# Value-product sums issued three half items earlier, the second dilated head held back until the values exist

## The chip, the cores and the metric

The kernel runs on one core of one Trainium2 chip. A core has a matrix engine (PE, TensorE), a vector engine (DVE), a scalar engine (ACT), a general engine (POOL) and an engine that issues DMAs (SP); each works through its own list of instructions in the order in which they stand there, and engines wait for each other by semaphores. The metric is the device time of one execution in microseconds (us), the median of several runs. Smaller is better.

## The reference

One decoder layer on x of 512 tokens by 1024 channels, in float32. A projection of x gives the queries, keys and values of three token mixers and three gates; the mixers' outputs are projected, gated, summed and projected again; a layer norm, an MLP with a gated embedding and a second layer norm follow. What matters here is the third mixer, dilated attention: 3 groups (g = 0, 1, 2) of 4 heads of 128 channels, combined over the groups by their softmax denominators.

```python
proj = x @ w_in
(da_q, da_k, da_v, sb_q, sb_k, sb_v, dl_q, dl_k, dl_v, gates) = jnp.split(proj, _split_points(), axis=-1)
...
o_dl = dilated_attention(dl_q.reshape(dil_shape), dl_k.reshape(dil_shape), dl_v.reshape(dil_shape),
                         rel_bias[:, DA_HEADS:])
...
# per group: logits = q k + bias, softmax over the window, o = prob @ v
wts = jax.nn.softmax(jnp.stack(lses, axis=0), axis=0)
o = wts[0][..., None] * outs[0] + wts[1][..., None] * outs[1] + wts[2][..., None] * outs[2]
```

## The kernel before

**Products in three parts.** A float32 operand is split into a high part (a rounded copy, made by ACT: lines 214 and 239) and a low part (the rest, made by DVE: lines 216 and 240). A product is then three matmuls: high by high, high by low, low by high. Weights come in chunks of 128x1024: SP loads a chunk into one of 7 buffers (`raw`), ACT makes `wh`, DVE makes `wl`, and PE uses them. There are 6 buffers each for `wh` and `wl`, so a chunk can be split only when PE is done with the chunk six places ahead of it.

**Items.** PE's main stream is a list of items, each a product over the whole depth with its weights. `item` records them, and the loop at the end of `trunk` goes through them. Between items, and once halfway through a whole item, the loop calls `step()`, which moves every unfinished attention head and every entry of `pending` on to its next `yield`. Half items (`size=0.5`), of which the values' products are made, have no halfway step. The place of a `yield` thus sets where the work after it is written among the items. From this written order a scheduling layer makes the final list of each engine, and it may move an instruction past others that do not depend on it. Tiles of 128x512 come out of one pool of 46 buffers (`slot`), so a tile may take the buffer of one that is no longer needed, and has to wait for its last reader.

**The values.** `value_pair` computes the dilated values of groups 1 and 2 with seven products in place of eight (Strassen's scheme, Winograd's form). They are numbered 1 to 7 and run in the order 2, 1, 7, 6, 4, 5, 3; each has two half items (r = 0, 1) of 12 matmuls. Products 2, 1 and 3 take x as it is. Products 7, 6, 4 and 5 take sums of blocks of x, which `value_forms` makes: it loads x again (`xr`, by POOL's DMA queue), waits some steps (`WAIT`), lets DVE form each sum in tiles `fr` (`o7`, `o6`, `o4`, `o1`, four instructions of 128x256 each), and `parts(p, ...)` splits it into a high part (`u7h`, ACT, line 239) and a low part (`u7l`, DVE, line 240). The sum called `o1` belongs to product 5, `o4` to product 4. Line 376 is the sum for 7, line 369 those for 6 and 4, line 388 that for 5.

**A dilated head.** `dil_head(hd)` is a generator, one for each of four heads. Head `hd` waits until its queries and keys of all three groups exist, then: the group 0 scores on PE (line 1589), DVE adds the bias and takes the maxima (1592), ACT takes the exponentials (1598); the scores of groups 1 and 2 (1605, 1613, 1620) likewise. Then each token's maxima and sums are exchanged between layouts by two small matmuls, `fold` (1630) and `foldT` (1632). On their output (`sel`, line 1636) DVE does a chain of small steps (1638 to 1652, with one exponential on ACT in it, 1647) which ends with the scaling of the exponentials (1654 and 1658). PE then transposes the scaled tiles (1673 for group 0, 1682 for groups 1 and 2), copies of them (`pt`) follow, and PE multiplies them by the values (1694, 1699). Before that last part a head waits for all values. Two heads can be under way together, since each counts 3 of 8 banks.

Of the kernel before, what the change touches and what calls it, by code (L numbers as in the profile page):

```python
# [57 lines left out]
def trunk(tc, a, out):  # L58
    nc = tc.nc
    es = ExitStack()  # L60
    with es:
# [14 lines left out]
        def slot(name, dt=F32):  # L76
            return big.tile([P, 512], dt, name=nm(name), tag="s", bufs=NSLOT)
# [176 lines left out]
        V = {}  # L254
# [89 lines left out]
        def form(to, p, r):  # L344
            fs = [split(r[kp], f"u{p}") for kp in range(2)]
            to[p] = [[fs[k // 2][i].rearrange("p (k t) -> p k t", k=2)[:, k % 2, :] for i in range(2)]
                     for k in range(4)]

        def value_forms():

            xr = [slot("xr") for _ in range(8)]
            for k, t in enumerate(xr):
                i = nc.gpsimd.dma_start(t, xt[:, k, :])
                tc.add_manual_dep(getattr(i, "ins", i), lows[-1].name, mybir.DependencyInfo(
                    mybir.DependencyClass.Sync, mybir.DependencyReason.DATA), reason="not ahead of time")

            def blk(kh, k, th):
                return xr[4 * kh + k].rearrange("p (t c) -> p c t", c=4)[:, 2 * th:2 * th + 2, :]

            def new():  # L360
                ts = [slot("fr") for _ in range(2)]
                return ts, [ts[k // 2].rearrange("p (k c t) -> p k c t", k=2, c=2)[:, k % 2] for k in range(4)]

            def parts(p, ts):
                form(vf, p, ts)
                vf[p] = [[(h[:, r * P:r * P + P], lo[:, r * P:r * P + P]) for r in range(2)] for h, lo in vf[p]]

            def neg_sub(o, i, j):
                nc.vector.scalar_tensor_tensor(o, i, -1.0, j, op0=OP.mult, op1=OP.subtract)

            for _ in range(WAIT):
                yield
            f7, o7 = new()
            with tc.issue_after(st["low"]):
                for k in range(4):
                    nc.vector.tensor_sub(o7[k], blk(1, k, 1), blk(0, k, 1))
            parts(7, f7)
            yield
            f6, o6 = new()
            with tc.issue_after(st["low"]):  # L380
                for k in range(4):
                    neg_sub(o6[k], o7[k], blk(0, k, 0))
            yield
            parts(6, f6)
            yield
            f1, o1 = new()
            for k in range(4):
                nc.vector.tensor_sub(o1[k], blk(0, k, 0), blk(0, k, 1))
            yield
            f4, o4 = new()  # L390
            for k in range(4):
                neg_sub(o4[k], o6[k], blk(1, k, 0))
            yield
            parts(4, f4)
            yield
            parts(5, f1)
            yield

        WAIT = 8

        def value_pair(nv):

# [1173 lines left out]
        def dil_head(hd):  # L1576
            while any(("dl_q", 4 * g + hd) not in T or ("dl_k", 4 * g + hd) not in T for g in range(3)):
                yield
            q = [T["dl_q", 4 * g + hd] for g in range(3)]
            k = [T["dl_k", 4 * g + hd] for g in range(3)]  # L1580
            stt = one.tile([P, 2, 8], F32, name=nm("st"), tag="st", bufs=4)
# [75 lines left out]
                o = L12[c // 2][:, (c % 2) * 256:(c % 2) * 256 + 256]  # L1657
                nc.vector.tensor_scalar(o, o, mxx[:, c:c + 1], None, op0=OP.mult)
            yield
            if hd < 2:  # L1660
                yield
                yield

# [48 lines left out]
        for hd in range(4):  # L1712
            waiting.append((3, dil_head(hd), DIL_PERIOD))
# [40 lines left out]
        for n, it in enumerate(items):  # L1754
# [4 lines left out]
            if n == v_from[0]:  # L1759
                pending.append(value_forms())  # L1760
# [182 lines left out]
```

## Time and profile before

| | |
|---|---|
| median of 3 runs | 1067.32 us (1067.2 to 1068.34) |
| the profiled execution | 1067.35 us, its span 1065.6 us |
| PE busy | 1049.0 us, 98% of the span |
| DVE busy | 774.1 us, 73% |
| ACT busy | 568.5 us, 53% |
| the values' seven products | from 238 to 295 us |
| dilated heads 0 and 1 | from 237 to 300 us; head 2 from 306, head 3 from 342 us |

Of the profile, three views are used. The table by stretches gives busy time of each engine in a stretch of time, with the granted clock of PE (PEclk, 1.00 is full) after the engines. The list of waits gives who waited for whom. The timeline gives instructions in order of time: start, duration, engine, line, operation, output and inputs, and in brackets how long the engine was idle before it and for whom it had waited. In the timeline a matmul of 128x512 has a duration near 0.4 us, but the next one starts 0.23 us after it: the starts tell how fast PE goes.

### The profile page before, as it was taken

The numbers are of one execution on the slowest core, as the hardware profiler recorded it, in microseconds if no ns is written. First come the engines' busy times: TensorE is split into PE (matmuls) and PEld (weight loads), VectorE is DVE, ScalarE is ACT, GpSimd is POOL, SyncE is SP. The second block draws the span as 40 slices with busy tenths as digits, with TensorE's granted clock in tenths as the row PEclk, the third lists the DMA queues.
The fourth block names the chain that finished last, engine by engine and source line by source line (L and its number), as shares of the span: only waits on it lengthen the run. The fifth ranks groups of instructions, "written<-read, shape, count | busy, mean of one in ns | idle before, by whom it ended". The sixth has DMA issues, their size and how long they took to land.

```text
span 1065.6 us, 15588 instructions
## 1 busy us (share of the span) xinstructions
PE 1049.0 (98%) x5802; PEld 905.1 (85%) x5802; DVE 774.1 (73%) x1383; ACT 568.5 (53%) x991; POOL 145.8 (14%) x224
## 2 busy tenths in 40 slices
PE   9999999999899999999999999999999999999996
PEld 6887788889788888888999988888999889889885
DVE  6887667649844757769768773888677877877965
ACT  6665445526432546547535452675756665666641
POOL 0001401220212103230111130100101100100000
PEclk9999999999899999999999999999999999999999
DMA  8346767974898819982676693148888978776602
GB/s 315 111 150 228 168 198 190 306 265 126 234 325 248 241 40 286 243 240 81 204 192 197 180 308 125 62 138 296 225 300 261 242 246 264 244 237 235 196 22 79
DMA packets 63260, 219.75 MB, mean 206 GB/s; under 512 B 7912, under 2 KB 8824, under 8 KB 63184
## 3 DMA queue, kind: packets, MB, share of 16 engines
q1 hardware_dynamic: 37056, 126.80, 34.1%
q0 software_dynamic: 25552, 91.04, 32.9%
q8 instruction: 45, 0.74, 0.3%
q10 hardware_dynamic: 576, 0.92, 0.2%
q14 instruction: 31, 0.25, 0.1%
HBM read 216.61 MB, written 81.81 MB: 280 GB/s over the span
## 4 chain that ended last, share of the span: by engine, by line
PE 88%; DVE 7%; issue 2%; ACT 2%; DMA 0%; POOL 0%; SPq 0%; DVEq 0%; POOLq 0%; ACTq 0%
PE mm L89 13%; PE mm L91 13%; PE mm L90 13%; PE at L89 4%; PE at L1076 4%; PE at L1077 4%; PE at L1078 4%; PE at L91 4%; PE at L90 4%; DVE wl L216 2%; PE mm L458 2%; PE mm L460 2%; PE mm L459 2%; PE at L133 1%; PE at L1467 1%
## 5 line engine op out<-in xcount | busy, mean ns | idle before, releaser
L214 ACT CAST wh<-raw 128x1024 fp32r<-128x1024 f32 x249 | 256.7, 1035 | 262.8 <-PE mm L90 158.7
L216 DVE TENSOR_TENSOR wl<-raw,wh 128x1024 fp32r<-128x1024 f32 x249 | 298.5, 1205 | 99.1 <-ACT wh L214 96.4
L89 PE MATMUL mm<-xhT,wh 128*128 128x512 f32 x368 | 146.7, 399 | 0.0
L91 PE MATMUL mm<-xhT,wl 128*128 128x512 f32 x368 | 144.4, 393 | 0.0
L90 PE MATMUL mm<-xlT,wh 128*128 128x512 f32 x368 | 144.0, 391 | 0.0
L91 PEld LDWEIGHTS mm<-xhT,wl 128*128 128x128 f32 x368 | 69.1, 188 | 15.0 <-DVE wl L216 0.3
L89 PEld LDWEIGHTS mm<-xhT,wh 128*128 128x128 f32 x368 | 69.2, 188 | 13.7 <-issue 0.4
L90 PEld LDWEIGHTS mm<-xlT,wh 128*128 128x128 f32 x368 | 69.2, 188 | 12.9
L1076 PE MATMUL at<-wh,hh 128*128 128x512 f32 x188 | 73.7, 392 | 0.0
L1077 PE MATMUL at<-wl,hh 128*128 128x512 f32 x188 | 73.7, 392 | 0.0
L89 PE MATMUL mm<-x1hT,wh 128*128 128x256 f32 x256 | 73.7, 288 | 0.0
L1078 PE MATMUL at<-wh,hl 128*128 128x512 f32 x188 | 73.1, 389 | 0.0
L90 PE MATMUL mm<-x1lT,wh 128*128 128x256 f32 x256 | 72.3, 283 | 0.0
L91 PE MATMUL mm<-x1hT,wl 128*128 128x256 f32 x256 | 71.9, 283 | 0.0
L89 PEld LDWEIGHTS mm<-x1hT,wh 128*128 128x128 f32 x256 | 48.8, 191 | 4.7 <-ACT up L1010 2.7
L90 PEld LDWEIGHTS mm<-x1lT,wh 128*128 128x128 f32 x256 | 48.9, 191 | 1.5
L914 POOL DMA_DIRECT2D usum<-in_wu_dram x32 | 28.5, 891 | 152.3 <-DVE wl L216 126.6
L91 PEld LDWEIGHTS mm<-x1hT,wl 128*128 128x128 f32 x256 | 48.6, 191 | 0.0
L914 POOL DMA_DIRECT2D dsum<-in_wd_dram x28 | 24.9, 890 | 130.9 <-DVE wl L216 96.2
L1078 PEld LDWEIGHTS at<-wh,hl 128*128 128x128 f32 x188 | 35.3, 188 | 7.7
L1076 PEld LDWEIGHTS at<-wh,hh 128*128 128x128 f32 x188 | 35.5, 189 | 6.0
L1077 PEld LDWEIGHTS at<-wl,hh 128*128 128x128 f32 x188 | 35.5, 189 | 5.5
(516 smaller groups left out, 2666.7 us busy)
## 6 DMA issues: line engine op xcount, KB each, us to landing
usum<-in_wu_dram POOLq DMA_DIRECT2D x48, 512.0 KB, 7.9
raw<-in_wt_dram SPq DMA_DIRECT2D x46, 512.0 KB, 5.1
dsum<-in_wd_dram POOLq DMA_DIRECT2D x42, 512.0 KB, 8.3
raw<-usum SPq DMA_DIRECT2D x32, 512.0 KB, 4.7
raw<-dsum SPq DMA_DIRECT2D x28, 512.0 KB, 4.5
raw<-in_wd_dram SPq DMA_DIRECT2D x25, 512.0 KB, 4.3
raw<-in_wu_dram SPq DMA_DIRECT2D x24, 512.0 KB, 5.2
raw<-in_wv_dram SPq DMA_DIRECT2D x18, 512.0 KB, 8.5
```

The costliest lines, as they stand in the source:

```text
L89: nc.tensor.matmul(ps, wh, xh, start=start, stop=False, skip_group_check=True)
L90: nc.tensor.matmul(ps, wh, xl, start=False, stop=False, skip_group_check=True)
L91: nc.tensor.matmul(ps, wl, xh, start=False, stop=stop, skip_group_check=True)
L214: i = nc.scalar.copy(h, raw)
L216: i = nc.vector.tensor_sub(lo, raw, h.bitcast(F32))
L458: nc.tensor.matmul(ps, x1, c["h"][:, s], start=k == 0, stop=False)
L459: nc.tensor.matmul(ps, x1, c["l"][:, s], start=False, stop=False)
L460: nc.tensor.matmul(ps, x2, c["h"][:, s], start=False, stop=k == 7)
L914: i = nc.gpsimd.dma_start(o, i, accum_op=OP.add, max_dma_last_dim=4096)
L1076: nc.tensor.matmul(ps, h[:, q], c["h"][:, s], start=go, stop=False, skip_group_check=True)
L1077: nc.tensor.matmul(ps, h[:, q], c["l"][:, s], start=False, stop=False, skip_group_check=True)
L1078: nc.tensor.matmul(ps, lo[:, q], c["h"][:, s], start=False, stop=end, skip_group_check=True)
```

## The change

Three edits. `WAIT` goes from 8 to 5, so `value_forms` starts three steps earlier. Inside it, the sum for product 4 and its split now come ahead of the sum for product 5. And head 1 of `dil_head` begins only when the last of the first pair's values exists; the two extra yields after the scaling, which heads 0 and 1 had, remain for head 0 alone.

```diff
             parts(6, f6)
             yield
+            f4, o4 = new()
+            for k in range(4):
+                neg_sub(o4[k], o6[k], blk(1, k, 0))
+            yield
+            parts(4, f4)
+            yield
             f1, o1 = new()
             for k in range(4):
                 nc.vector.tensor_sub(o1[k], blk(0, k, 0), blk(0, k, 1))
             yield
-            f4, o4 = new()
-            for k in range(4):
-                neg_sub(o4[k], o6[k], blk(1, k, 0))
-            yield
-            parts(4, f4)
-            yield
             parts(5, f1)
             yield
 
-        WAIT = 8
+        WAIT = 5
...
+            while hd == 1 and ("dl_v", 1, 3) not in V:
+                yield
...
-            if hd < 2:
+            if hd == 0:
                 yield
                 yield
```

The lines of `dil_head` from the new wait on are three higher afterwards (1632 becomes 1635, 1673 becomes 1676).

Where instructions now stand. The first place is DVE's list at the low part of the sum for product 4 (`u4l`). Before, it stands behind the chain of head 1 (`sel_2597` to `mxx_2602`, `ex_2604`):

```order
L369 SCALAR_TENSOR_TENSOR fr_2656<-fr_2480,xr_2186 128x256
L1643 TENSOR_TENSOR mxx_2602<-st_2459,ot_2599 128x8
L369 SCALAR_TENSOR_TENSOR fr_2656<-fr_2480,xr_2187 128x256
L1645 TENSOR_TENSOR ex_2604<-st_2459,mxx_2602 128x8
...
L216 TENSOR_TENSOR wl_2713<-raw_2294,wh_2712 128x1024
L1650 TENSOR_TENSOR mxx_2602<-mxx_2602,ex_2604 128x8
L240 TENSOR_TENSOR u4l_2692<-fr_2656,u4h_2691 128x512
```

Now it stands right behind the maxima of head 0 and ahead of that head's `foldT` operand (`r_517`), and all of `sel` and what follows comes later:

```order
L1626 TENSOR_TENSOR r_516_2475<-st_2408,exf 128x32
L240 TENSOR_TENSOR u4l_2480<-fr_2429,u4h_2479 128x512
L1620 TENSOR_SCALAR nm_2423<-st_2408 128x4
L216 TENSOR_TENSOR wl_2501<-raw_2051,wh_2500 128x1024
L240 TENSOR_TENSOR u4l_2484<-fr_2430,u4h_2483 128x512
L216 TENSOR_TENSOR wl_2507<-raw_2119,wh_2506 128x1024
L1629 TENSOR_TENSOR r_517_2477<-st_2408,exf 128x32
L436 TENSOR_TENSOR dl_v_2448<-dl_v_2448,mm_2548 128x512
L1639 TENSOR_TENSOR sel_2518<-at_2515,pick 128x64
L436 TENSOR_TENSOR dl_v_2512<-dl_v_2512,at_2573 128x512
L1641 TENSOR_REDUCE ot_2520<-sel_2518 128x2x4
```

The sums for product 4 have moved ahead of the work that they stood behind. The second place is PE's list at head 0's `foldT` (line 1632) and its first transposes (line 1673). Before, a product 1 half item less two matmuls (`mm_2577`), a whole one (`at_2627`) and one of product 7 (`mm_2662`, inputs `u7h` and `u7l`) stand between the two:

```order
L1632 MATMUL at_2514<-r_509_2457,foldT 128x32
L428 MATMUL mm_2577<-wh_2235,xlT 128x512
...
L1630 MATMUL at_2594<-r_536_2565,fold 128x32
L426 MATMUL at_2627<-wh_2235,xhT 128x512
...
L426 MATMUL mm_2662<-wh_2337,u7h_2407 128x512
...
L428 MATMUL mm_2662<-wh_2371,u7l_2412 128x512
L1673 MATMUL at_2678<-ident,L_490_2381 128x128 x3
```

Now both half items of product 1 and five of product 7's first twelve matmuls stand ahead of `foldT` (now line 1635), and seven matmuls stand between it and the transposes (now line 1676):

```order
L427 MATMUL mm_2602<-wl_2352,u7h_2331 128x512
L1635 MATMUL at_2515<-r_517_2477,foldT 128x32
L428 MATMUL mm_2602<-wh_2351,u7l_2332 128x512
L426 MATMUL mm_2602<-wh_2399,u7h_2335 128x512
L427 MATMUL mm_2602<-wl_2400,u7h_2335 128x512
L428 MATMUL mm_2602<-wh_2399,u7l_2336 128x512
...
L1676 MATMUL at_2618<-ident,L_502_2409 128x128 x3
```

The number of matmuls between `foldT` and the first transpose went from 34 to 7 (a small `fold` of head 1 aside). On DVE, between head 0's `sel` and its scaling (line 1657), there now stand one addition for product 1 and two weight chunks' low parts:

```order
L1639 TENSOR_TENSOR sel_2518<-at_2515,pick 128x64
L436 TENSOR_TENSOR dl_v_2512<-dl_v_2512,at_2573 128x512
L1641 TENSOR_REDUCE ot_2520<-sel_2518 128x2x4
L1643 TENSOR_REDUCE ot_2520<-sel_2518 128x2x4
L216 TENSOR_TENSOR wl_2587<-raw_2176,wh_2586 128x1024
L1646 TENSOR_TENSOR mxx_2523<-st_2408,ot_2520 128x8
L216 TENSOR_TENSOR wl_2593<-raw_2239,wh_2592 128x1024
L1648 TENSOR_TENSOR ex_2525<-st_2408,mxx_2523 128x8
```

Before, head 1's maxima (line 1613) and one low part stood there. The third place is PE's list behind the values, where head 1 now begins (`at_2871`) with head 2 right behind it (`at_2981`); before, head 1 was over by then and head 2 was there alone:

```order
L1592 MATMUL at_2871<-dl_k_1532,dl_q_1488 128x128
...
L1633 MATMUL at_2949<-r_619_2924,fold 128x32
L1592 MATMUL at_2981<-dl_k_2178,dl_q_2121 128x128
L1592 MATMUL at_2981<-dl_k_2178,dl_q_2121 128x256
L1592 MATMUL at_2982<-dl_k_2178,dl_q_2121 128x256 x2
L1635 MATMUL at_2949<-r_620_2926,foldT 128x32
L89 MATMUL mm_2997<-xhT,wh_2751 128x512
```

Head 1's `foldT` now stands behind head 2's first scores, and 20 matmuls of the next item (`mm_2997`) stand between it and head 1's transposes. From the fourth item behind the values on, PE's list is the same as before.

More of the change, by code (lines that the diff above doesn't have):

```diff
@@ L385, in value_forms @@
             yield
-            f1, o1 = new()
-            for k in range(4):
-                nc.vector.tensor_sub(o1[k], blk(0, k, 0), blk(0, k, 1))
-            yield
             f4, o4 = new()
@@ L395, in value_forms @@
             yield
+            f1, o1 = new()
+            for k in range(4):
+                nc.vector.tensor_sub(o1[k], blk(0, k, 0), blk(0, k, 1))
+            yield
             parts(5, f1)
             yield
-        WAIT = 8
+        WAIT = 5
         def value_pair(nv):
```

## The prediction

> **What bounds the kernel now.** I read the page's head first, then the list of PE's waits, then the timeline where those waits lie, then the table by stretches for the clock.
>
> ```profile
> span 1065.6 us, 15588 instructions
> PE 1049.0 (98%) x5802; PEld 905.1 (85%) x5802; DVE 774.1 (73%) x1383; ACT 568.5 (53%) x991; POOL 145.8 (14%) x224
> ```
>
> PE is busy 98% of the span: a change gains only where PE idles or runs slowly, and loses where it makes PE do so. The two longest of PE's waits stand in one place:
>
> ```profile
> PE mm L426 <- ACT u4h L239: 2.1, 1, 2.1
> PE mm L428 <- DVE u4l L240: 1.5, 1, 1.5
> ```
>
> PE waited for the high and the low part of the sum for product 4. The timeline of PE there, with earlier rows that serve as its prices:
>
> ```profile
> 258.77 0.93 PE L1673 MATMUL at<-ident,L 128*128 128x128 f32 x7
> 259.45 0.47 PE L426 MATMUL at<-wh,u7h 128*128 128x512 f32 x1
> ...
> 263.92 0.41 PE L1632 MATMUL at<-r,foldT 128*128 128x32 f32 x2
> 264.16 0.48 PE L428 MATMUL mm<-wh,u6l 128*128 128x512 f32 x1
> 264.48 0.39 PE L426 MATMUL mm<-wh,u6h 128*128 128x512 f32 x1
> 264.71 0.40 PE L427 MATMUL mm<-wl,u6h 128*128 128x512 f32 x1
> ...
> 266.08 0.40 PE L428 MATMUL mm<-wh,u6l 128*128 128x512 f32 x1
> 268.53 0.50 PE L426 MATMUL mm<-wh,u4h 128*128 128x512 f32 x1 [2.06 <-ACT u4h L239]
> 268.87 0.40 PE L427 MATMUL mm<-wl,u4h 128*128 128x512 f32 x1
> 270.78 0.79 PE L428 MATMUL mm<-wh,u4l 128*128 128x512 f32 x1 [1.52 <-DVE u4l L240]
> ...
> 276.36 0.38 PE L1682 MATMUL at<-ident,L 128*128 128x128 f32 x2
> ```
>
> Starts are 0.23 us apart (264.48 to 264.71), and seven transposes take 0.68 (258.77 to 259.45). From 266.08 to 276.36 PE did one matmul, the twelve of product 4's first half and seven transposes: 13 x 0.23 + 0.68 = 3.67 us of work in 10.28. So 6.6 us are lost there. Of these 2.2 and 1.7 are pauses (266.31 to 268.53, 269.10 to 270.78); the other 2.7 is a slow clock:
>
> ```profile
> 268.00:270.00 2.00, 0.73 (x2) 0.30 (x2) 2.00 (x6) 1.98 (x4) 0.00 (x0) 0.79 1.03 279
> 270.00:272.00 2.00, 1.22 (x3) 1.03 (x4) 2.00 (x7) 0.00 (x0) 1.65 (x2) 0.50 0.56 160
> ...
> 274.00:276.00 2.00, 2.00 (x8) 1.60 (x7) 1.25 (x4) 0.00 (x0) 0.00 (x0) 0.50 1.06 211
> 276.00:278.00 2.00, 2.00 (x17) 1.84 (x16) 1.44 (x3) 1.10 (x2) 0.00 (x0) 1.00 1.03 256
> ```
>
> The granted clock is 0.50 from about 269.2 (a mean of 0.79 over 2 us) to 276, some 6.8 us. DVE, busy for all 2.00 us of these stretches until 274, is what was late.
>
> **The change part by part.** It adds no work and removes none; it moves three things.
>
> *The sums earlier (8 to 5, and 4 ahead of 5).* By DVE's new order the sum for 4 and both its low parts stand right behind head 0's maxima, some twenty microseconds ahead of PE's use of them (268.53 above). The waits of 2.2 and 1.7 us go, and the slow clock that came of them: **-6.6 us**. What can be late next is the start: the earliest sum now stands in DVE's list behind the low part that ended at 227.1, and reads x loaded anew:
>
> ```profile
> 214.36 4.26 POOL L353 DMA_DIRECT2D xr<-in_xT_dram  x8 [5.74 <-DVE wl L216]
> ...
> DMA to landing us min/median/max: 5.2/6.1/7.2
> ...
> 225.91 1.23 DVE L216 TENSOR_TENSOR wl<-raw,wh 128x1024 fp32r<-128x1024 f32 x1 [0.17 <-ACT wh L214]
> 230.00:240.00 10.00, 10.00 (x46) 8.63 (x45) 4.32 (x11) 2.70 (x3) 1.37 (x2) 1.00 0.51 145
> ```
>
> The last xr is issued by 218.6 and lands by 225.8 at the slowest, 1.3 us ahead. The early sums cost nothing, since DVE is busy only 4.32 of the 10 us from 230; if the loads came later than 227.1, DVE would stand, but PE, with other operands in hand, not at once. No DMA is added, and the loads keep their place on POOL's queue; SP's loads follow DVE's low parts, most of which move by a microsecond or less.
>
> *Head 0 has its `foldT` later.* This is the new cost. `foldT` now stands behind both halves of product 1, and only seven matmuls separate it from the transposes that need DVE's whole chain. How long that chain is, heads 2 and 3 show:
>
> ```profile
> 316.40 0.31 PE L1632 MATMUL at<-r,foldT 128*128 128x32 f32 x2
> 320.46 1.14 PE L1673 MATMUL at<-ident,L 128*128 128x128 f32 x7
> ...
> 316.75 0.22 DVE L1636 TENSOR_TENSOR sel<-at,pick 128x64 f32<-128x64 f32 x1 [0.78 <-PE at L1632]
> 317.26 1.21 DVE L216 TENSOR_TENSOR wl<-raw,wh 128x1024 fp32r<-128x1024 f32 x1
> 318.39 0.16 DVE L1643 TENSOR_TENSOR mxx<-st,ot 128x8 f32<-128x8 f32 x1
> 320.03 1.08 DVE L1654 TENSOR_SCALAR L<-L,mxx 128x128 f32<-128x128 f32 x4
> ...
> 352.93 0.30 PE L1632 MATMUL at<-r,foldT 128*128 128x32 f32 x2
> 358.48 1.28 PE L1673 MATMUL at<-ident,L 128*128 128x128 f32 x7 [0.17 <-DVE L L1654]
> ...
> 265.02 0.70 DVE L436 TENSOR_TENSOR dl_v<-dl_v,at 128x512 f32<-128x512 f32 x1
> ```
>
> In head 2 it took 4.06 us from `foldT` (316.40) to the first transpose (320.46), with one foreign low part of 1.13 in it (317.26 to 318.39): 2.9 bare. In head 3 it took 5.55 with more strangers, and PE did wait, so such a chain sets PE's start. In the new order head 0's chain holds two low parts and one addition (0.65, from the row of 0.70 less its overlap): 2.9 + 2 x 1.13 + 0.65 = 5.8; some gaps between dependent small steps are filled by the strangers, which I put at 0.2: 5.6. PE meanwhile has `foldT` and the first matmul behind it (264.48 - 263.92 = 0.56) and six more at 0.23: 1.9. So PE stands **3.6 us**, ahead of the seven transposes. Bounds: 3.2 if the strangers fill more, 4.3 if `foldT`'s own operand, which now also follows the sum for 4 and two low parts, is late too. I take 3.6, from the sum.
>
> *The clock after it.* No row shows one pause of 3.6 us. Below, a pause that leaves the clock alone: 0. Above, 6.8 us at half clock all spent on work: 6.8 x 2.7 / 5.2 = 3.5, since the 5.2 us of slow work from 270.78 to 276 cost 2.7. The nearest row is that one, as the pauses total about the same (3.9 us against 3.6). I take **2.1**, a little less than 2.7, because the old pause came in two parts, and the clock could not begin to recover until 1.6 us after its drop (269.2 to 270.78), while unbroken work follows the new one.
>
> [...]
>
> *Head 1 behind the values.* Its work is the same but moves from a stretch where DVE is full to one where it is not:
>
> ```profile
> 300.00:310.00 10.00, 10.00 (x49) 8.44 (x49) 2.64 (x10) 2.59 (x6) 1.61 (x2) 1.00 1.05 353
> ```
>
> DVE is busy there 2.64 of 10 us. Head 1's own chain there holds one low part (1.13) and head 2's four maxima (about 1.3): 2.9 + 2.4 = 5.3, less 0.3 of filled gaps, 5.0. PE has 0.56 and 19 x 0.23 = 4.9 in that time. **+0.1**; bounds 0 and 1. There are also fewer changes between small and large matmuls on PE, each of which costs about 0.1 (264.16 to 264.48 is 0.32 in place of 0.23), some four fewer: **-0.4**. The two yields dropped for head 1 cost nothing, as its transposes lie where PE has the items' work; if that cover went, they would be part of the same 0.1. Waiting ahead of head 1 stand no instructions: the wait is one in the writing order, not on an engine. Heads 2 and 3 keep their turn.
>
> **Sum.** -6.6 + 3.6 + 2.1 + 0.1 - 0.4 = -1.2. The profiled execution took 1067.35 us (a span of 1065.6 and 1.75 around it), 0.03 above the median of the three runs. That gives 1066.1.
>
> **The rivals.** Same, within 0.2%, means within 2.1 us here, about what a measurement tells from no change.
>
> 1. *The new stall does not come:* head 0's scaling is done when PE reaches the transposes. It would need the chain in 1.9 us, and the bare one is 2.9 already; only if DVE or PE ran elsewhere than by their lists. Then -6.6 - 0.4 = -7.0: 1060.3. Chance 0.07.
>
> 2. *The stall comes, but the clock stays:* -1.2 - 2.1 = -3.3: 1064.0. For it speaks that a pause of 2.2 us alone preceded the old drop by less than one more us of work, so that a pair of pauses may have been needed; against it, that the new pause is longer than either. Chance 0.22.
>
> 3. *Slower: head 1 stalls PE behind the values as head 0 does.* Place: its transposes, 20 matmuls behind its `foldT`. The margin is nil (5.0 against 4.9), and head 2's first work sits in its chain. From 3.3 us more than I count it outweighs the gain and the bound of 2.1; a full repetition, a pause of 3.6 and a slow clock of 2.1, gives -1.2 + 5.7 = +4.5: 1071.9. Against it: DVE is three quarters idle there. Chance 0.13.
>
> 4. *The change does nothing:* the 6.6 us return elsewhere in full, as another wait for the sums. DVE's list speaks against it; it would be 1067.4, inside the same verdict. Chance 0.06.
>
> **How the numbers follow.** My forecast has 0.52, from 1064.9 (clock 1.0) to 1067.9 (clock 3.0, stall 4.3); a tenth of it counts as faster, the rest as same. Faster, below 1065.2: 0.07 + 0.22 + 0.05 = 0.34, to which I add 0.03 for small terms that all fall well, 0.37. Slower: 0.13 + 0.01. Same: 0.49. The range for 8 in 10 takes in rival 2 and part of 3: 1063.4 to 1068.6; the forecast's own is 1064.9 to 1067.9.
>
> **What would show it.** Right: no wait for `u4h` or `u4l` in PE's list; one wait of 3 to 4 us at the first transposes of head 0 near 255 to 259 us, for DVE's scaling, with `sel` 0.35 us behind `foldT` and two low parts in between; a granted clock of 0.50 for some microseconds after it; no wait above 0.5 us at heads 1 and 2. Wrong: a clock of 1.00 behind that pause takes 2.1 off, a second wait behind the values adds; and any wait in the first product 7 half would say that the early sums were not early enough.

## The result and the profile after

The changed kernel takes **1065.72 us** (median) against 1067.05 for the kernel before, each over 22 executions: a ratio of 0.999, with a 95% interval of 0.9983 to 0.9996. The forecast was 1066.1 with "within 0.2%" as the likeliest case, and the difference lies within that. The profiled execution took 1065.99 us, 1.36 less than that of before. One execution after (2100.37 us) and one of experiment 1 (1288.95 us) were in a slow state and stand in no ratio.

The head of the page after:

```profile
span 1064.3 us, 15603 instructions
PE 1046.7 (98%) x5802; PEld 903.7 (85%) x5802; DVE 776.6 (73%) x1383; ACT 568.9 (53%) x991; POOL 146.2 (14%) x224
```

In the list of PE's waits those for `u4h` and `u4l` are gone, and one of 3.5 us stands in their place:

```profile
PE at L1676 <- DVE L L1657: 3.7, 2, 3.5
```

PE's timeline around it (start, duration, line, output and inputs; the idle time before in brackets):

```profile
253.35 0.30 PE L1635 MATMUL at<-r,foldT 128*128 128x32 f32 x2
...
254.95 0.39 PE L428 MATMUL mm<-wh,u7l 128*128 128x512 f32 x1
258.88 1.14 PE L1676 MATMUL at<-ident,L 128*128 128x128 f32 x7 [3.54 <-DVE L L1657]
259.77 0.48 PE L426 MATMUL at<-wh,u7h 128*128 128x512 f32 x1
...
261.06 0.63 PE L427 MATMUL at<-wl,u7h 128*128 128x512 f32 x1
261.49 0.63 PE L428 MATMUL at<-wh,u7l 128*128 128x512 f32 x1
...
264.20 1.03 PE L1685 MATMUL at<-ident,L 128*128 128x128 f32 x8
264.99 0.48 PE L426 MATMUL mm<-wh,u6h 128*128 128x512 f32 x1
```

This is head 0: `foldT` at 253.35, its transposes at 258.88. After the pause matmuls start 0.43 us apart (261.06 to 261.49) in place of 0.23. From 254.95 to 264.99 PE did 13 matmuls, seven transposes and eight more (0.79): 2.99 + 0.68 + 0.79 = 4.46 us of work in 10.04. The loss is 5.6 us, 3.7 of it the pause (254.95 + 0.23 to 258.88). It replaces the old loss of 6.6.

What DVE did meanwhile:

```profile
253.69 0.22 DVE L1639 TENSOR_TENSOR sel<-at,pick 128x64 f32<-128x64 f32 x1 [0.79 <-PE at L1635]
253.83 0.68 DVE L436 TENSOR_TENSOR dl_v<-dl_v,at 128x512 f32<-128x512 f32 x1
...
254.66 1.22 DVE L216 TENSOR_TENSOR wl<-raw,wh 128x1024 fp32r<-128x1024 f32 x1
...
255.87 1.22 DVE L216 TENSOR_TENSOR wl<-raw,wh 128x1024 fp32r<-128x1024 f32 x1
...
258.45 1.07 DVE L1657 TENSOR_SCALAR L<-L,mxx 128x128 f32<-128x128 f32 x4
```

One addition and two low parts stand inside the chain from `sel` to the scaling. The granted clock (the third number from the end of each row, a mean over 2 us):

```profile
260.00:262.00 2.00, 2.00 (x8) 1.52 (x7) 2.00 (x6) 0.86 (x2) 0.00 (x0) 0.61 1.08 297
262.00:264.00 2.00, 2.00 (x7) 1.57 (x6) 1.92 (x4) 1.54 (x3) 0.00 (x0) 0.54 1.03 266
264.00:266.00 2.00, 2.00 (x14) 1.74 (x13) 1.75 (x3) 2.00 (x5) 0.13 (x1) 1.00 0.46 182
```

Half clock held for (1 - 0.61) x 4 + (1 - 0.54) x 4 = 3.4 us, where it had been 6.8 before. Head 1, behind the values, does not stall PE: no idle time stands before its transposes.

```profile
300.92 0.30 PE L1635 MATMUL at<-r,foldT 128*128 128x32 f32 x2
305.69 0.81 PE L1676 MATMUL at<-ident,L 128*128 128x128 f32 x5
```

### The profile page after: what moved, and what is told of

Same layout as the page of the kernel before. It is cut to its first block, busy times and chain, and to the rows that moved or that the text cites. A ratio compares the mean times of both kernels' runs of the same rounds, so it can differ in the third digit from the quotient of the medians.

```text
span 1064.3 us, 15603 instructions
## 1 busy us (share of the span) xinstructions
PE 1046.7 (98%) x5802; PEld 903.7 (85%) x5802; DVE 776.6 (73%) x1383; ACT 568.9 (53%) x991; POOL 146.2 (14%) x224
## 4 chain that ended last, share of the span: by engine, by line
PE 88%; DVE 6%; issue 2%; ACT 2%; DMA 0%; POOL 0%; SPq 0%; DVEq 0%; POOLq 0%; ACTq 0%
PE mm L89 13%; PE mm L91 13%; PE mm L90 13%; PE at L89 4%; PE at L1077 4%; PE at L1076 4%; PE at L1078 4%; PE at L91 4%; PE at L90 4%; DVE wl L216 2%; PE mm L458 2%; PE mm L460 2%; PE mm L459 2%; PE at L1467 1%; PE at L133 1%
```

## The experiments

Ratios are against the kernel before, run beside each experiment, with the 95% interval. The medians of before in these sets lie between 1066.5 and 1066.8 us, so a few tenths of a us between two experiments mean nothing. Each code cut is a difference from the changed kernel, and `...` marks lines left out. The expectations call the reading of the prediction theory A: the earlier sums remove the old loss, and head 1's move crowds head 0's chain. Theory B: it is head 1's leaving that removes it.

**1. The sums' two edits alone.**

```diff
-            while hd == 1 and ("dl_v", 1, 3) not in V:
-                yield
...
-            if hd == 0:
+            if hd < 2:
                 yield
                 yield
```

> The sums' two edits alone (WAIT 5, the sum for product 4 ahead of that for 5), head 1 as in the kernel before. Theory A: it is the earlier sums that take away the old loss of 6.6 us (two waits for u4h and u4l and the slow clock after them), and head 1's move is what crowds head 0's chain. In this order head 0 has 26 matmuls (6.5 us) between foldT and its transposes, and its chain holds two foreign low or sum steps (1.3 us) and some of head 1's maxima (about 2.2): 2.9 + 3.5 = 6.4, so no stall; head 1 has 22 matmuls and 15 transposes (about 7 us) against a chain of 2.9 + 3 x 1.13 + 3 x 0.65 = 8.2: a wait of about 1 us. So 1067.1 - 6.6 + 1 = 1061.5, up to 1063 if the clock falls after it. Theory B: the old loss goes because head 1's chain leaves DVE's full stretch, not because of the sums: then this kernel keeps DVE as full as before, some wait for u4h, u4l or a head of 3 us or more remains and the time is 1065 to 1067.

Measured: 1066.86 us, ratio 1.000 (0.9991 to 1.0009). No wait for `u4h` or `u4l` is left, and head 0's transposes don't wait. But PE stands at head 1's `fold`, for the operand `r` (PE's and DVE's timelines):

```profile
260.03 0.49 PE L1631 MATMUL at<-r,fold 128*128 128x32 f32 x2 [3.76 <-DVE r L1624]
```
```profile
257.49 1.07 DVE L1655 TENSOR_SCALAR L<-L,mxx 128x128 f32<-128x128 f32 x4
258.47 1.13 DVE L1659 TENSOR_SCALAR L<-L,mxx 128x256 f32<-128x256 f32 x4
259.52 0.34 DVE L1614 CUSTOM_DVE_ANT_0 L<-at,shf,ma 128x128 f32<-128x128 f32 x1
...
259.79 0.18 DVE L1624 TENSOR_TENSOR r<-st,exf 128x32 f32<-128x32 f32 x1
```

Head 1's last maximum (259.52) stands behind head 0's scalings (257.49 and 258.47), and `r` behind that. The earlier sums do remove the old waits, as theory A has it, but the time they free is spent at the next work that DVE has late: the time and the wait of more than 3 us at a head are what theory B expected. The place that I expected, head 1's transposes, was wrong.

**2. Head 1's edit alone.**

```diff
-        WAIT = 5
+        WAIT = 8
...
+            f1, o1 = new()
+            for k in range(4):
+                nc.vector.tensor_sub(o1[k], blk(0, k, 0), blk(0, k, 1))
+            yield
             f4, o4 = new()
...
-            f1, o1 = new()
-            for k in range(4):
-                nc.vector.tensor_sub(o1[k], blk(0, k, 0), blk(0, k, 1))
-            yield
             parts(5, f1)
```

> Head 1's edit alone (it waits for the values, its two extra yields dropped), the sums as in the kernel before. Theory A: the sums for product 4 stand late on DVE as before, so the waits for u4h and u4l stay, 2 us or more in all, with a slow clock: 1065 to 1067. Theory B: DVE is free of head 1's chain and reaches the sums for product 4 in time, so no wait for u4h or u4l; what is left is head 0: 14 matmuls (3.9 us) between foldT and transposes against a chain of 2.9 + 2 x 1.13 + 2 x 0.65 - 0.3 = 6.2, a wait of 2.3 to 2.7 us, and half clock for one 3.4 us window behind it (1.6): 1067.1 - 6.6 + 2.5 + 1.6 = 1064.6; 1063.0 if the clock stays.

Measured: 1063.42 us, ratio 0.997 (0.9958 to 0.9982). No wait for the sums for 4; one of 2.0 us at head 0's transposes, and the clock stays at 1.00. PE's timeline, then DVE's, then the table by stretches:

```profile
257.04 0.87 PE L1676 MATMUL at<-ident,L 128*128 128x128 f32 x5 [2.03 <-DVE L L1657]
...
267.55 0.39 PE L428 MATMUL mm<-wh,u4l 128*128 128x512 f32 x1
```
```profile
266.63 0.68 DVE L240 TENSOR_TENSOR u4l<-fr,u4h 128x512 fp32r<-128x512 f32 x1
```
```profile
258.00:260.00 2.00, 2.00 (x11) 1.72 (x10) 1.77 (x5) 0.98 (x3) 0.00 (x0) 1.00 1.07 279
```

`u4l` is done at 267.31, 0.24 us ahead of PE. Theory B holds: head 1's edit alone removes the old loss, and it is worth more than the whole change. On top of it the sums' edits cost 0.2%: 0.997 becomes 0.999.

**3. Head 0's transposes further behind.** The changed kernel with

```diff
-            if hd == 0:
-                yield
-                yield
+            for _ in range(5 if hd == 0 else 0):
+                yield
```

> The changed kernel with head 0's transposes put five steps behind its scaling in place of two; nothing else. 43 matmuls (10.1 us) stand between foldT and the first transposes in place of 7. DVE's chain also takes in the four sums for product 5, one low part of it and one more weight chunk (2.2 + 0.65 + 1.13): 5.6 + 4.0 = 9.6. Theory A (the new loss is the short distance from foldT to the transposes, 3.54 us of wait plus about 1.6 us of half clock): both go, 1065.7 - 5.1 = 1060.6, and no clock of 0.50 near 260 us. Rival: DVE is simply short of time there, and the wait turns up at a later place (u5, u6 or the transposes): more than 1063.5.

Measured: **1060.18 us**, ratio 0.9939 (0.9927 to 0.9952), the fastest of all. No wait is left between 230 and 330 us. PE's timeline and DVE's:

```profile
252.99 0.30 PE L1635 MATMUL at<-r,foldT 128*128 128x32 f32 x2
...
263.09 0.93 PE L1675 MATMUL at<-ident,L 128*128 128x128 f32 x7
```
```profile
261.05 1.11 DVE L1657 TENSOR_SCALAR L<-L,mxx 128x128 f32<-128x128 f32 x4
```

The first scaling ends at 262.16, PE comes at 263.09, and the clock is 1.00 throughout this part. Against the change that is 5.5 us less, where its loss of 5.6 stood. Its five executions lie within 0.13 us of each other; the 16 of before that ran beside them spread over 1.9.

**4. The sums one step earlier, not three** (`WAIT = 7`, the rest as in the change).

> The changed kernel with WAIT 7 in place of 5 (the sums one step earlier than before the change, not three). foldT of head 0 then has 25 matmuls (6.2 us) to its first transposes, and the chain holds one addition and three low parts: 2.9 + 0.65 + 3 x 1.13 = 6.9. The sums for product 4 stand behind head 0's scaling. Theory A in the strict form (the sums must be three steps earlier to be in time): a wait for u4h or u4l of 1 us or more comes back, 1063 to 1066. Theory B (with head 1 out of the way the sums are in time in either place): no wait for u4h or u4l, a wait of 0.7 us at the transposes, too short for the clock: 1067.1 - 6.6 + 0.7 = 1061.2.

Measured: 1062.44 us, ratio 0.996 (0.9948 to 0.9973).

```profile
256.21 0.87 PE L1676 MATMUL at<-ident,L 128*128 128x128 f32 x5 [0.60 <-DVE L L1657]
...
278.03 0.63 PE L426 MATMUL at<-wh,xhT 128*128 128x512 f32 x1 [0.72 <-DVE dl_v L447]
```

The wait at the transposes is 0.60, as worked out (0.7), and none is for the sums. A second of 0.72 appears, for DVE's last step on product 5, which I had not counted. The three steps are not needed with the two yields.

**5. Experiment 2 with five steps for head 0.**

```diff
-        WAIT = 5
+        WAIT = 8
...
-            if hd == 0:
-                yield
-                yield
+            for _ in range(5 if hd == 0 else 0):
+                yield
```

(and the sum for 5 ahead of that for 4.)

> Head 1's edit and head 0's transposes five steps behind the scaling, with the sums where they were before the change (WAIT 8, the sum for 5 ahead of that for 4). Theory B (the earlier sums add nothing once head 1 is out of the way): PE has 50 matmuls (11.7 us) between head 0's foldT and its transposes, no wait there, none for u4h or u4l: 1060.2, as the run with the earlier sums and five yields. Theory A (the earlier sums are worth something even then): a wait of 1 us or more for u6, u4 or u5, and 1061.5 or more.

Measured: 1062.23 us, ratio 0.9959 (0.9946 to 0.9973). PE's and DVE's timelines:

```profile
265.52 0.51 PE L428 MATMUL mm<-wh,u4l 128*128 128x512 f32 x1 [1.18 <-DVE u4l L240]
```
```profile
259.40 2.18 DVE L388 TENSOR_TENSOR fr<-xr 128x256 f32<-128x256 f32 x4
261.49 2.23 DVE L369 SCALAR_TENSOR_TENSOR fr<-fr,xr 128x256 f32<-128x256 f32 x4
263.64 1.22 DVE L216 TENSOR_TENSOR wl<-raw,wh 128x1024 fp32r<-128x1024 f32 x1
264.78 0.69 DVE L240 TENSOR_TENSOR u4l<-fr,u4h 128x512 fp32r<-128x512 f32 x1
```

With PE no longer held at head 0, it reaches product 4 before `u4l`. So here theory A holds: against experiment 3 the later sums cost 2 us, of which this wait is 1.2; no wait in the profile names the rest. The same edits that cost 2 us with two yields bring 2 us with five.

**6. Head 0's chain made longer.**

```diff
             nc.vector.reciprocal(mxx, mxx)
+            for _ in range(8 if hd == 0 else 0):
+                nc.vector.tensor_scalar(mxx, mxx, 1.0, None, op0=OP.mult)
```

> The changed kernel with head 0's chain made 1.6 us longer: eight multiplications by 1 behind the reciprocal, each about 0.2 us from start to start in the profile after. If PE's wait there is set by the chain alone, it goes from 3.5 to 5.1 us and the time rises by 1.6 at least: 1067.3. On the clock: if a pause of one piece costs one stretch of half clock whatever its length, that stays 3.4 us and the time is 1067.3; if the slow stretch grows with the pause to 6.8 us, as before the change, it costs 1.6 more: 1068.9. If something else than the chain held PE, the time stays below 1066.5.

Measured: 1067.68 us, ratio 1.0007 (0.9998 to 1.0016), 2.0 above the change. DVE's and PE's timelines, and the stretches:

```profile
258.04 1.61 DVE L1656 TENSOR_SCALAR mxx<-mxx 128x8 f32<-128x8 f32 x8
```
```profile
260.32 1.73 PE L1678 MATMUL at<-ident,L 128*128 128x128 f32 x7 [5.19 <-DVE L L1659]
```
```profile
258.00:260.00 2.00, 0.00 (x0) 0.00 (x0) 1.66 (x11) 0.00 (x0) 0.00 (x0) 0.82 1.03 299
260.00:262.00 2.00, 1.68 (x8) 1.70 (x9) 2.00 (x9) 0.00 (x0) 0.00 (x0) 0.50 1.07 293
...
266.00:268.00 2.00, 2.00 (x14) 1.69 (x14) 1.50 (x2) 2.00 (x4) 0.67 (x2) 0.98 0.00 0
```

The wait grew by 1.65 for 1.61 us of added chain: the chain alone holds PE there. Half clock now lasts from about 259.3 to 266.1, 6.8 us, but its first microsecond falls into the pause; the time lies between the two that were expected.

**7. The old order of the sums in the change.**

```diff
+            f1, o1 = new()
+            for k in range(4):
+                nc.vector.tensor_sub(o1[k], blk(0, k, 0), blk(0, k, 1))
+            yield
             f4, o4 = new()
...
-            f1, o1 = new()
-            for k in range(4):
-                nc.vector.tensor_sub(o1[k], blk(0, k, 0), blk(0, k, 1))
-            yield
             parts(5, f1)
```

> The changed kernel with the sum for product 5 ahead of that for product 4 again (WAIT 5 and head 1's edit stay). The order of PE's list changes: 22 matmuls (5.5 us) stand between head 0's foldT and its transposes in place of 7, as products 6 and 4 are drawn ahead. The chain holds one low part of a sum, two of weights, two additions and one step more: 2.9 + 0.65 + 2.26 + 1.3 + 0.6 = 7.7, so a wait of 2 us at the transposes; waits for u4l ahead of it would come on top. Theory A (the order of the sums is needed against the old wait): a wait for u4h or u4l of 1 us or more, 1064 or more. Theory B (it isn't): the wait at the transposes alone, 1062.5, or 1064 with a slow clock.

Measured: 1061.84 us, ratio 0.9953 (0.9941 to 0.9966).

```profile
253.45 0.30 PE L1635 MATMUL at<-r,foldT 128*128 128x32 f32 x2
...
259.42 0.50 PE L426 MATMUL mm<-wh,u4h 128*128 128x512 f32 x1 [1.08 <-DVE dl_v L440]
...
260.23 0.27 PE L1676 MATMUL at<-ident,L 128*128 128x128 f32 x1
```

No wait for `u4h` or `u4l`, and none at head 0's transposes, where I had worked out 2 us. PE stood 1.08 just before, for DVE's addition to product 6, and came to the transposes that much later (260.23), so this pause covers what the chain would have cost there. The chain was also shorter than worked out: at most 260.23 - 253.45 = 6.8 us from `foldT` (253.45), not 7.7. By the time it is theory B. Undoing the order gains 3.9 us; with it PE's list changes too, and 22 matmuls stand between `foldT` and the transposes, not 7.

**8. Head 1 keeps its two extra yields** (`if hd < 2:` again, the rest as in the change).

> The changed kernel with head 1's two extra yields kept. The prediction put their loss at nothing. Heads 0's place is the same, so the 3.5 us of wait and its clock stay; behind the values head 1's transposes move from 20 matmuls behind its foldT to 43. Theory (they cost nothing): 1065.7 within 0.5. Rival (head 1's transposes, now later, meet those of heads 2 and 3, 22 in a row, and its copies or banks hold PE): 1066.5 or more.

Measured: 1066.09 us, ratio 0.9991 (0.9982 to 1.0), the same as the change (0.9983 to 0.9996). Head 0's wait is 3.54 again. Dropping the yields costs nothing, as predicted.

**9 and 10. Head 0 with three and with four steps** (`range(3 ...)`, `range(4 ...)` in experiment 3).

> As the run with five steps behind head 0's scaling, but three. DVE's list up to the scaling is the same as with five, where the chain took 9.2 us from foldT (252.99) to the end of the first scaling (262.16); PE has 27 matmuls between foldT and the transposes in place of 43: 0.56 + 26 x 0.23 = 6.5. So a wait of 2.7 us: 1060.2 + 2.7 = 1062.9 if the clock stays, as it did after a pause of 2.03; 1064.5 if one stretch of half clock follows, as after 3.54. If the distance in matmuls is not what sets the wait, there is none and the time is 1060.2.

> The same with four steps: 31 matmuls between foldT and the transposes, 0.56 + 30 x 0.23 = 7.5 us against a chain of 9.2: a wait of 1.7 us, which is too short for the clock: 1061.9. If the distance doesn't set the wait: 1060.2.

Measured: 1062.69 us, ratio 0.9959 (0.9946 to 0.9973), and 1062.39 us, ratio 0.9955 (0.9942 to 0.9967). The times are near those expected, the mechanism is not: the wait is 1.62 in both, and not at the transposes. PE's and ACT's timelines in experiment 9, and the same copy in the change:

```profile
259.73 0.50 PE L426 MATMUL mm<-wh,u6h 128*128 128x512 f32 x1 [1.62 <-ACT dl_v L437]
```
```profile
256.79 1.05 ACT L214 CAST wh<-raw 128x1024 fp32r<-128x1024 f32 x1 [2.37 <-PE at L428]
...
258.14 1.04 ACT L214 CAST wh<-raw 128x1024 fp32r<-128x1024 f32 x1 [0.19 <-PE at L428]
259.10 0.58 ACT L437 COPY dl_v<-mm 128x512 f32<-128x512 f32 x1
```
```profile
261.13 0.59 ACT L437 COPY dl_v<-mm 128x512 f32<-128x512 f32 x1 [3.64 <-DVE fr L394]
```

Product 6 needs the bank that holds product 1's first half, which ACT copies out. In ACT's list that copy stands behind two weight casts, and these wait for PE to free a buffer. In the change the copy came later still (261.13, behind DVE's sum for product 5, line 394), but PE, held at the transposes, began product 6 only at 264.99, so it cost nothing. With five steps the other half of product 6 comes first in PE's list, and the copy is hidden again. Each set against the before beside it, the two are 2.2 and 2.0 us above experiment 3; 1.6 of that is this wait, and the rest I cannot place.

**11. The order without the earlier start** (`WAIT = 8`, the rest as in the change).

> The changed kernel with WAIT back at 8: the sum for 4 ahead of that for 5, and head 1's edit. PE's list is that of the run with head 1's edit alone around head 0 (14 matmuls between foldT and the transposes), and so is DVE's chain. If the changed order of the sums costs only where it comes with the earlier start (by drawing head 0's foldT down to seven matmuls), this run equals that one: a wait of 2.0 us at the transposes and 1063.4. If the order costs by itself: 1064.5 or more.

Measured: 1063.64 us, ratio 0.997 (0.9958 to 0.9981): the same as experiment 2.

```profile
257.69 0.87 PE L1676 MATMUL at<-ident,L 128*128 128x128 f32 x5 [2.06 <-DVE L L1657]
```

The order costs nothing by itself; it costs where it comes with the earlier start. Of the two on top of head 1's edit, the earlier start without the order (experiment 7) is the better by the medians, 0.9953 against 0.997, though the intervals touch.

**12. Experiment 11 with five steps for head 0.**

> The run with head 1's edit and five steps for head 0 at WAIT 8 had one wait left, 1.18 us for u4l, and took 1062.2. Here the one thing added is the order of the sums: 4 ahead of 5. The four sums for 5 (2.2 us on DVE) no longer stand ahead of u4l. If that order is what the earlier sums were worth there, the wait goes and the time is 1060.2 to 1061.0; if it is the earlier start (WAIT 5) that matters, it stays at 1061.9 or more, with a wait for u4l or another of 1 us.

Measured: 1062.19 us, ratio 0.9958 (0.9944 to 0.9972). The wait for `u4l` is gone, but another has come:

```profile
278.73 0.63 PE L426 MATMUL at<-wh,xhT 128*128 128x512 f32 x1 [0.70 <-DVE dl_v L447]
```

So the order alone does not bring the 2 us; the earlier start is needed for them. This wait is 0.7 of the 2 us, and no wait names the rest. Whether the earlier start would bring them without the order, no run shows.

## Why the prediction was right, and where its reasons were not

*The sum.* Every term came out near its size:

| term | predicted | measured |
|---|---|---|
| old loss around product 4 | -6.6 | gone |
| wait at head 0's transposes | +3.6 | +3.7 (3.54 by the wait) |
| the clock after it | +2.1 | +1.9 (5.6 less the pause), 1.6 of it the clock |
| heads 1 and 2, changes of kind | -0.3 | -0.6 (what is left) |

The last row was not measured by itself. Where PE's two lists agree ahead of the dilated heads, it was 0.08 us later than before (236.68 against 236.60), and behind them 1.48 us earlier (327.33 against 328.81). That is a gain of 1.56, of which 6.6 - 5.6 = 1.0 is accounted for above. The 1.6 of the clock is from the twelve matmuls behind the transposes: 4.43 us (259.77 to 264.20) where 12 x 0.23 = 2.76 would do, less 0.1 for the change of kind.

The chain from `foldT` to the transposes took 258.88 - 253.35 = 5.53 us (5.6 predicted), with the strangers that were named, `sel` 0.34 behind `foldT`, and `r` not late. Head 1 took 4.77 us from `foldT` to its transposes without a wait (4.9 for PE).

*The clock.* The term was of about the right size, but not for the reason given. As 5.2 us of slow work had cost 2.7 before, 2.1 stands for about 4.0 us at half clock. What came was half as long as before, 3.4 us for 6.8, and it began 1.6 us behind the end of the pause (258.88 to 260.44). The prediction's reason, a clock that recovers sooner where unbroken work follows one pause, no run shows: in experiment 6 unbroken work followed one pause too, from 260.32 on, and half clock lasted 6.8 us, 5.8 of it behind the pause. That the size came so near is thus in part luck. The mean granted clock of the executions suggests that both lengths occur: four of them at 0.994 took 1066.56 to 1067.09, the others at 0.995 or 0.996 1065.12 to 1066.16. The rounded mean alone does not part them, as the profile of before, with 6.8 us at half clock, has 0.995. None took less than 1065.12, and without the half clock 1.6 less than 1065.7 would be expected, so rival 2 did not come true. In experiment 8, with the same pause in its profile (3.54), two of eleven executions at 0.997 took 1063.79 and 1064.26, close to the 1064.0 of that rival, which suggests that it occurs there, if rarely.

*Where it failed.* The step "The waits of 2.2 and 1.7 us go, and the slow clock that came of them: -6.6 us" puts the gain down to the sums, and the step "Head 1 behind the values" puts +0.1 beside it. That pricing of edits one by one is wrong. Alone, the sums gain nothing (1.000) and head 1's edit 0.3% (0.997). Either takes the old waits away; what differs is which chain DVE is then late with. And of what the prediction calls the new cost of head 0's later `foldT`, a wait of 2.03 us comes with head 1's edit alone (experiment 2) and 2.06 with the new order as well (11); only the order and the earlier start together make it 3.54 and bring the half clock. The total was right because the new wait was worked out from the final order of both lists, where the parts had already met, and because the term for the clock fell near, in part by luck.

*The other rivals.* 1 (no new stall) did not occur in the change, and experiment 3 shows its price: 1060.2 against the 1060.3 worked out. 3 (head 1 stalls PE) did not occur. 4 (the loss comes back in full, as another wait for the sums) did not occur in the change; the sums' edits alone come near it in time, but there the wait is for `r`.

## What to carry to other kernels

Where PE is nearly always busy and another engine sits in a chain with it, count what PE has between the instruction that starts the chain and the one that needs its end, and what strangers the other engine has in between: that gave the waits at head 0's transposes within 0.7 us, as long as nothing else stopped PE first (as in experiments 7, 9 and 10). Edits that move work on the same engine are not additive; price the final order, and try each edit alone before keeping all. And when a stall is removed, look for work that was late behind its cover: here waits of 1.6 us for a copy, 0.7 for a last step and 1.2 for a sum each came to light that way.

## What the runs showed of the hardware

Among the values' products half clock lasted 3.4 or 6.8 us in the profiles. Single pauses of 0.60, 0.70, 0.72, 1.08, 1.18, 1.62, 2.03 and 2.06 us left the clock up: the profiled executions that had them (experiments 2, 4, 5, 7 and 9 to 12) have a mean granted clock of 0.997, as that of experiment 3, which has none between 230 and 330 us. Behind the pause of 2.03 the clock is 1.00 from 256 to 262 us, and behind that of 2.06 in experiment 11 matmuls start 0.23 us apart (259.33 to 259.56). Pauses of 3.54 (the change and experiment 8) and 3.76 us (experiment 1) brought 3.4 us at half clock: in experiment 8 means of 0.69, 0.50 and 0.96 over the 2 us stretches from 258 to 264, so (0.31 + 0.50 + 0.04) x 4 = 3.4, and in experiment 1 0.56 and 0.59 from 260 to 264, so (0.44 + 0.41) x 4 = 3.4. The pause of 5.19 us in experiment 6, and the pair of 2.06 and 1.52 before the change, brought 6.8.

The length of the pause alone does not decide. Before the change the clock fell at about 269.2 (a mean of 0.79 from 268 to 270), when only the pause of 2.06 was over (268.53), while those of 2.03 and 2.06 in experiments 2 and 11 left it up. One execution of experiment 11, at a mean clock of 0.995 and 1.1 us above the next (1064.96 against 1063.85), suggests that it can fall there too. This rests on one profile of each kernel; what decides beside the length, the runs don't settle.
